# A hybrid decoder layer on one core: index scores in three float32r products, the lead in halves, new ranks

## The chip, the cores and the metric

The kernel runs on one core of a Trainium2 chip. The metric is the device time of one execution in microseconds (us), taken as the median over runs. PE is the matrix engine TensorE, PEld its weight loads, DVE is VectorE, ACT is ScalarE, POOL is GpSimd, and SP issues the transfers.

## The reference, cut to what matters

One decoder layer over 1024 tokens of width 1024. The input is RMS-normalised, scaled and shifted by vectors computed from a conditioning vector `c`, and projected to 2888 columns. Half of the mixed width comes from a pooling mixer with windows 2, 4, 8 and 16, half from sparse attention: an indexer scores every key for every query, the 256 best keys are kept, and attention runs over those.

```python
mod = jnp.einsum('bd,de->be', jax.nn.silu(c), w_ada[l]) + b_ada[l]
shift, scale, gate = jnp.split(mod, 3, axis=-1)
h = rms_norm(x, norm_w[l]) * (1.0 + scale[:, None, :]) + shift[:, None, :]
proj = jnp.einsum('bsd,de->bse', h, w_in[l])
...
logits = jnp.einsum('bqhd,bsd->bqhs', qib, kf_idx) * (IDX_DIM ** -0.5)
score = jnp.einsum('bqhs,bqh->bqs', jax.nn.relu(logits), wb) * (N_IDX_HEADS ** -0.5)
score = jnp.where(causal[None], score, -jnp.inf)
_, sel = lax.top_k(score, k_top)
...
y = jnp.einsum('bse,ed->bsd', jnp.concatenate([pool_out, attn_out], axis=-1), w_out[l])
x = x + gate[:, None, :] * y
```

The indexer has 8 heads of 64 dimensions and one shared key. Queries 0 to 255 keep all their keys, so scores are computed for the query tiles 2 to 7 (128 queries each) alone.

## The kernel before

Every strand of work is a Python generator that yields instructions one by one. At build time a list scheduler (`Flow`) decides which strand's next instruction is issued to its engine; it goes by a model of each instruction's length and by ranks, the numbers in `EARLY`, `LAST` and `SAFE`, and by the order of the projection tiles in `ORDER`. Each engine then runs its instructions in that fixed order. `Either(...)` lets the scheduler choose the engine. A `bank` is one of eight PSUM banks of 512 columns; the constants `QK`, `IK`, `FK`, `PV` and `KEEP` say how many banks a strand must leave free. All instructions pass through one helper, so that they have one line number in the profile, and the names of tiles tell them apart.

Matmuls in float32 accuracy are made of three products in the single-pass type float32r: a tile is split in a high part (a rounded copy) and a low part (the rest), and high x high, low x high and high x low are added in PSUM. For the normalised input the parts are `hhi` and `hlo`, for the weights `wh` and `wl`. The index scores and the attention scores are an exception before the change: they are plain f32 matmuls over 64 dimensions (`kiT,qix` and `kT,qr`), two heads at a time, one on the upper and one on the lower 64 rows of the array.

In the order of time:

1. Squares of the input blocks (`sq`) are summed over the width by 64 one-column matmuls (`c,sq`). `token_scales` makes of them one factor for each token, spread over all partitions (`rsb`). DVE computes `scale` and `shift` by products with accumulation (`wa`), each followed by a small operation on a column (`c<-c`).
2. The lead (`lead_line`): the eight input blocks are normalised on the fly (`xn`, `hhi`, `hlo`, by `h_block`), and each is multiplied with its chunk of weights as soon as it is there. The key/value matmuls (`wkh`, `wkl`) follow.
3. `index_keys` turns the index keys (`kiT`); `index_scores` issues the score matmuls, ACT takes their relu (`kt<-m`, a ring of two tiles), DVE sums them with the head weights (`score`). The other projections (`etile`: `hhi,wh`, `hhi,wl`, `hlo,wh`, 512 columns each) fill PE between them.
4. The 256th largest score of each query is found by bisection over 16-bit keys: DVE does it for the query tiles 2 to 4 (one round is three counts `junk`, a compare `aq` and a step `xq`), ACT for 5 to 7 (`ajunk`). Meanwhile DVE sums shifted copies `nx` for the pooling mixers, whose results `u` PE multiplies (`u,c`), and `qsh`/`qsl` split the queries for their norms.
5. Attention: scores `kT,qr`, masked maxima (`ex`, `mx`), exponentials, transposes (`c,ex`, `pw`), products with the values (`pw,vrow`). The output projections (`mph`, `mpl` for the mixers, `mah`, `mal` for attention) fill PE.

Of the kernel before, what the change touches and what calls it, by code (L numbers as in the profile page):

```python
# [17 lines left out]
P = 128  # L18
# [9 lines left out]
ORDER = "a2 a0 a1 q1 q2 | q0 m1 q3 m3 m2 m0 a3"  # L28
SWAP16 = [(i + 16) % 32 for i in range(32)]
WARM = [()] * 8  # L30
# [8 lines left out]
EARLY = {"main": 0.6, "fill": 0.4, "weights": 0.0, "evac": -1.0, "side": 0.2, "h": -0.2, "mods": -0.2,  # L39
         "select": -0.1, "scores": -0.6, "attend": -1.1, "late": 1.0, "kv": -0.3, "qi": -0.8, "pick": -0.6,  # L40
         "mix": -0.36, "rotated": -0.18, "query_loads": 0.01, "exps": -0.11, "score_sums": -1.13,
         "key_value_out": -0.58, "index_queries": -1.39, "norm": -2.29, "gate_loads": -0.03, "token_scales": -0.31,
         "gate_mods": 0.58, "unit": -0.41, "index_scores": -0.39, "lead_loads": 1.53, "out": -1.53, "lead_out": -0.72,
         "weight_loads": -0.1, "key_value_weights": -0.24, "main_line": 1.04, "output_line": 0.3, "turns": -1.82,
         "finish": -0.62, "index_keys": -0.9, "h_block": -0.1, "attention_keys": -0.68, "turned": -1.72,
         "h_blocks": -0.05, "gated": -1.24}

SELECT = -0.461
LAST = {"main": 0.12, "fill": 0.129, "scores": 0.008}

SAFE = {"side": 1.0, "unit": 0.1, "query_norms": 0.67, "rotated": 0.7, "norm": 0.45, "weight_loads": 0.1}

SCALED = (0,)
# [3 lines left out]
WKM = 4  # L57
# [3 lines left out]
PHOP = -0.008  # L61
STT = 0.062
HOPS = {"PE": 0.19, "DVE": 0.13, ("ACT", "DVE"): 0.14, ("ACT", "ACT"): 0.035}

SWITCH = {"all": 0.1, "rows": 0.25, "columns": 0.32}
# [3 lines left out]
PW_POOL = 0.4  # L69
XO_POOL = 0.45  # L70
BACK = 0.5
SPAN = 0.5

QK = 4
IK = 4
FK = 2
# [3 lines left out]
KEEP = 6  # L80
# [3 lines left out]
PV = 2  # L84

WA_AHEAD = 5
AHEAD = 3
XN_AHEAD = 2

FAVOUR = {"DVE": 0.122, "ACT": -0.13, "POOL": 0.013}  # L90
# [9 lines left out]
class Op:  # L100
# [29 lines left out]
    def _cost(self, aps, kw):  # L130
# [5 lines left out]
        if eng == "PE":  # L136
            rate = 2 if self.name == "transpose" else 4 if aps[1].dtype == F32 else 1
            if rate == 4 and min(aps[0].shape[0], aps[1].shape[0]) == 64:
                self.mode = "rows" if aps[1].shape[0] == 64 else "columns"
                rate = 2  # L140
            return max(0.109, size[0] * 0.000417 * rate + 0.0135)
# [128 lines left out]
class Flow:  # L270
# [3 lines left out]
    def __init__(self):  # L274
# [5 lines left out]
        self.strands = []  # L280
# [47 lines left out]
    def spawn(self, gen, kind="side"):  # L328
        s = [gen, EARLY.get(gen.__name__, EARLY[kind]), None, kind]
# [45 lines left out]
def hybrid_layer(ctx, tc, xT, cT, nwT, badaT, wada, wq, wet, wkv, qnw, knw, wpool,  # L375
# [79 lines left out]
    sc = const([P, 8], F32)  # L455
    rs = const([P, 8], F32)
# [1064 lines left out]
```

## Time and profile before

| what | value |
|---|---|
| median of 3 runs | 534.77 us (533.91 to 534.86) |
| profiled execution: time | 535.14 us |
| profiled execution: span | 533.2 us |
| PE busy | 510.2 us, 96% of the span |
| DVE busy | 427.3 us, 80% |
| ACT busy | 376.4 us, 71% |
| POOL busy | 160.5 us, 30% |

The span is the time from the first to the last instruction that the trace records; 1.9 us of the profiled execution lie around it. PE counts as busy for nearly the whole span, but busy time is counted at whatever clock is granted, so a stretch at half clock counts as busy too.

### The profile page before, as it was taken

Reading aid. Unit: us, or ns where it says so; the run is one execution under the profiler, and the core shown is the slowest. Engines: PE = TensorE matmul, PEld = TensorE weight load, DVE = VectorE, ACT = ScalarE, POOL = GpSimd, SP = SyncE. Lnnn points to the kernel's source line nnn. Section 1 sums busy time; section 2 is a strip of 40 time slices with the busy share of each in tenths; the row PEclk is TensorE's granted clock in tenths of the full one; section 3 lists DMA queues with packets and bytes.
Section 4 is the critical chain, followed back from the end, with each engine's and each line's share of the span. In section 5 each row is a group of like instructions: output and inputs, shape, how many; then the busy total and the mean of one; then the engine's idle time right before and its main releaser. Section 6 shows DMA issues by size and latency. Waiting matters only on the chain.

```text
span 533.2 us, 7630 instructions
## 1 busy us (share of the span) xinstructions
PE 510.2 (96%) x2492; PEld 378.2 (71%) x2492; DVE 427.3 (80%) x895; ACT 376.4 (71%) x848; POOL 160.5 (30%) x173
## 2 busy tenths in 40 slices
PE   5969999999999999999999797999999999999997
PEld 5758899755657887878878575876585856636575
DVE  0699996699886899999999899798856999886142
ACT  6357731487878888999962789799999834796420
POOL 1298240000000345555246147243202423100000
PEclk9979999999999999999999798899999999999999
DMA  8995418202011111121110014465252723301044
GB/s 307 405 408 167 136 48 297 79 0 80 21 61 59 41 41 41 39 71 49 36 44 20 21 60 125 131 188 182 69 177 81 227 90 100 98 20 41 1 157 158
DMA packets 28023, 58.29 MB, mean 109 GB/s; under 512 B 3792, under 2 KB 7888, under 8 KB 27984
## 3 DMA queue, kind: packets, MB, share of 16 engines
q1 hardware_dynamic: 27984, 57.81, 31.8%
q8 instruction: 19, 0.31, 0.3%
q14 instruction: 20, 0.16, 0.1%
HBM read 47.32 MB, written 10.49 MB: 108 GB/s over the span
## 4 chain that ended last, share of the span: by engine, by line
PE 55%; DVE 31%; ACT 6%; issue 5%; DMA 1%; POOL 1%; SPq 0%; DVEq 0%; POOLq 0%
PE m L196 55%; DVE junk L196 9%; ACT ex L196 4%; DVE ex L196 3%; DVE selw L196 3%; DVE aq L196 2%; DVE nx L196 1%; DVE sw L196 1%; DVE xq L196 1%; DVE key L196 1%; DVE wa L196 1%; DVE u L196 1%; DVE hlo L196 1%; DVE qr L196 1%; DVE gp L196 1%
## 5 line engine op out<-in xcount | busy, mean ns | idle before, releaser
L196 PE MATMUL m<-hhi,wh 128*128 128x512 f32 (+1 forms) x320 | 120.8, 399 | 0.5 <-ACT hhi L196 0.5
L196 PE MATMUL m<-hlo,wh 128*128 128x512 f32 (+1 forms) x320 | 114.8, 383 | 4.5 <-DVE hlo L196 4.5
L196 PE MATMUL m<-hhi,wl 128*128 128x512 f32 (+1 forms) x320 | 115.7, 383 | 0.0
L196 ACT ACTIVATE ajunk<-key,xq 128x768 bf16<-128x768 uint16 (+2 forms) x93 | 96.4, 1037 | 4.9 <-DVE xq L196 3.6
L196 PEld LDWEIGHTS m<-hhi,wh 128*128 128x128 f32 x320 | 59.6, 191 | 21.0 <-issue 7.4
L196 POOL TENSOR_TENSOR wl<-ld,wh 128x512 fp32r<-128x512 f32 x40 | 61.6, 1542 | 33.8 <-ACT wh L196 15.3
L196 PEld LDWEIGHTS m<-hlo,wh 128*128 128x128 f32 x320 | 59.2, 190 | 16.9 <-DVE hlo L196 5.2
L196 DVE TENSOR_SCALAR_CACHE_REDUCE junk<-key,xq 128x384 bf16<-128x384 uint16 (+2 forms) x93 | 69.1, 743 | 2.2
L196 PEld LDWEIGHTS m<-hhi,wl 128*128 128x128 f32 x320 | 59.5, 191 | 12.9 <-issue 1.9
L196 ACT ACTIVATE ex<-ex,mx,c 128x256 f32<-128x256 f32 (+7 forms) x64 | 54.8, 858 | 2.2 <-DVE mx L196 2.1
L196 ACT ACTIVATE kt<-m 128x512 f32<-128x512 f32 (+1 forms) x80 | 38.0, 523 | 13.3 <-DVE score L196 9.5
L196 DVE SCALAR_TENSOR_TENSOR score<-kt,c,score 128x1024 f32<-128x1024 f32 (+5 forms) x42 | 39.9, 950 | 6.7 <-ACT kt L196 4.8
L196 PE MATMUL m<-kT,qr 64*128 64x512 f32 (+3 forms) x192 | 39.0, 515 | 3.5 <-DVE mx L196 3.5
L196 DVE CUSTOM_DVE_ANT_0 ex<-m,key 128x512 f32<-128x512 f32 (+1 forms) x48 | 30.9, 661 | 6.3 <-PE m L196 6.3
L196 PEld LDWEIGHTS m<-c,ex 128*128 128x128 f32 x288 | 31.7, 140 | 5.9 <-ACT ex L196 2.8
L196 PE MATMUL m<-c,ex 128*128 128x128 f32 x288 | 35.1, 275 | 0.8 <-ACT ex L196 0.8
L196 DVE SCALAR_TENSOR_TENSOR xo<-m,c,xo 128x512 f32<-128x512 f32 x23 | 17.0, 740 | 22.6 <-PE m L196 22.3
L196 PEld LDWEIGHTS m<-kT,qr 64*128 64x128 f32 x192 | 18.2, 188 | 22.6 <-issue 12.2
L196 PE MATMUL m<-pw,vrow 128*64 128x512 f32 x144 | 33.5, 601 | 0.0
L196 PE MATMUL m<-kiT,qix 64*128 64x512 f32 (+3 forms) x160 | 32.2, 532 | 0.0
L196 POOL TENSOR_SCALAR_AFFINE_SELECT score<-score 128x128 f32<-128x128 f32 x6 | 3.1, 510 | 91.1 <-PE m L196 46.5
L196 ACT CAST wh<-ld 128x512 fp32r<-128x512 f32 x35 | 21.4, 617 | 11.2 <-PE m L196 11.2
(182 smaller groups left out, 1050.7 us busy)
## 6 DMA issues: line engine op xcount, KB each, us to landing
wa<-wada SPq DMA_DIRECT2D x24, 512.0 KB, 7.5
ld<-wet SPq DMA_DIRECT2D x16, 512.0 KB, 3.3
ld<-wout SPq DMA_DIRECT2D x24, 256.0 KB, 2.8
xo<-xT SPq DMA_DIRECT2D x16, 256.0 KB, 3.3
y_d<-xo SPq DMA_DIRECT2D x16, 256.0 KB, 2.3
xo<-y_d SPq DMA_DIRECT2D x16, 256.0 KB, 3.0
outT<-xo SPq DMA_DIRECT2D x16, 256.0 KB, 2.1
xt<-xT SPq DMA_DIRECT2D x7, 512.0 KB, 6.9
```

Of the source, the lines that this page charges most:

```text
L196: self.fn(*self.args, **self.kw)
```

## The change

Three things change together. First, index queries and index keys are split in high and low parts (`split` on the queries gives `xh` and `xl`; `turn_split` gives two tiles `kiT`), and each f32 score matmul becomes three float32r products (`dots`), issued alternately for the two row groups. Second, in the lead the token sums go to two banks, one for each half of the tokens, with scales per half; the first block is normalised in halves (`first_block`), the small column operations become strands of their own that may run on ACT or DVE (`gear`, `shift`), and two filler matmuls (`xt,c`) go. Third, ranks, model constants and bank reserves get new values, many ranks per instance of a strand.

```diff
-ORDER = "a2 a0 a1 q1 q2 | q0 m1 q3 m3 m2 m0 a3"
+ORDER = "a0 a2 a1 q1 q2 | q0 m1 q3 m2 m3 m0 a3"
...
-SCALED = (0,)
...
+SCALED = ()
...
-WKM = 4
+WKM = 5
...
-QK = 4
-IK = 4
-FK = 2
+QK = 3
+IK = 3
+FK = 0
...
-KEEP = 6
+KEEP = 7
...
-PV = 2
+PV = 3
...
-AHEAD = 3
+AHEAD = 2
...
-        s = [gen, EARLY.get(gen.__name__, EARLY[kind]), None, kind]
+        name = gen.__name__
+        n = self.spawned[name] = self.spawned.get(name, 0) + 1
+        s = [gen, EARLY.get(f"{name} {n}", EARLY.get(name, EARLY[kind])), None, kind]
...
+        halves = [slice(512, 1024), slice(0, 512)]
+        tab["sums"] = []
+        for _ in range(2):
+            tab["sums"].append((yield bank(4)))
+        added = [j for j in range(NT) if j not in SUMS]
+        acc, started = None, set()
         for j in range(NT):
             sq = yield big(s="sq")
-            for c in ([slice(0, 512), slice(512, 1024)] if j == NT - 1 else [slice(0, 1024)]):
+            for c in (halves if j == NT - 1 else [slice(0, 1024)]):
                 yield A.activation(sq[:, c], xt[j][:, c], AF.Square)
-                if acc is not None and j not in SUMS:
+                if j in added and acc is not None:
                     yield V.tensor_tensor(acc[:, c], acc[:, c], sq[:, c], op=OP.add)
-                if j == NT - 1 or j in SUMS:
+                if j in SUMS or j == added[-1]:
                     t = sq if j in SUMS else acc
-                    for b in range(c.start // P, c.stop // P):
-                        yield mm(ps_r[:, b:b + 1], t[:, b * P:(b + 1) * P], ones, j == SUMS[0] and b == 0,
-                                 j == NT - 1 and b == NT - 1)
+                    for h, half in enumerate(halves):
+                        if half.start >= c.start and half.stop <= c.stop:
+                            for b in range(4):
+                                o = half.start + b * P
+                                yield mm(tab["sums"][h][:, b:b + 1], t[:, o:o + P], ones,
+                                         h not in started, j == NT - 1 and b == 3)
+                                started.add(h)
...
+        for h, r in enumerate((rs[:, 4:8], rs[:, 0:4])):
+            yield A.activation(r, tab["sums"][h], AF.Sqrt, scale=1.0 / 1024.0, bias=eps_sb)
+            flow.drop(tab["sums"][h])
+            yield V.reciprocal(r, r)
+            ps = yield bank()
+            yield Group([PE.transpose(ps[:, b * P:(b + 1) * P], r[:, b:b + 1].to_broadcast([P, P]), ident)
                          for b in range(4)])
-        tab["ps_b"] = ps_b
-        for half in range(2):
-            yield A.copy(rsb[:, half * 512:(half + 1) * 512], ps_b[half])
+            rsbs.append(ps)
...
+            yield V.scalar_tensor_tensor(ada[j][0], ada[j][0], 1.0, tab["scp"], op0=OP.mult, op1=OP.mult, accum_out=g)
             flow.drop(ada[j][0])
-            yield V.tensor_scalar(gs[:, j:j + 1], m, bada_sb[:, 8 + j:9 + j], nw_sb[:, j:j + 1],
-                                  op0=OP.add, op1=OP.mult)
-            geared.append(j)
-            yield from modulation(ada[j][1], tab["scp"], j)
-            modded.append(j)
+            flow.spawn(gear(j, g), "mods")
+            yield V.scalar_tensor_tensor(ada[j][1], ada[j][1], 1.0, tab["scp"], op0=OP.mult, op1=OP.mult, accum_out=m)
+            flow.drop(ada[j][1])
+            flow.spawn(shift(j, m), "mods")
...
+    def gear(j, g):
+        yield Either(A.activation(gs[:, j:j + 1], g, AF.Identity, scale=nw_sb[:, j:j + 1], bias=bnw[:, j:j + 1]),
+                     V.tensor_scalar(gs[:, j:j + 1], g, bada_sb[:, 8 + j:9 + j], nw_sb[:, j:j + 1],
+                                     op0=OP.add, op1=OP.mult))
+        geared.append(j)
+
+    def shift(j, m):
+        b = bada_sb[:, j:j + 1]
+        yield Either(A.activation(m, m, AF.Identity, bias=b), V.tensor_scalar(m, m, b, None, op0=OP.add))
+        modded.append(j)
...
+    def first_block():
+
+        xn = yield big(s="xn")
+        hi = yield big(F32R, s="hhi")
+        lo = yield big(F32R, s="hlo")
+        g, m = gs[:, 0:1], mod_sb[:, 0:1]
+
+        def low(n, c):
+            yield V.scalar_tensor_tensor(lo[:, c], xn[:, c], m, hi[:, c].bitcast(F32), op0=OP.add, op1=OP.subtract)
+            lo_in.append((0, n))
+            hlo[0] = lo
+            if len(lo_in) == 2:
+                flow.drop(xn)
+
+        for n, c in enumerate((slice(512, 1024), slice(0, 512))):
+            yield lambda: len(rsbs) > n and 0 in geared
+            yield V.scalar_tensor_tensor(xn[:, c], xt[0][:, c], g, rsbs[n], op0=OP.mult, op1=OP.mult)
+            yield lambda: 0 in modded
+            yield A.activation(hi[:, c], xn[:, c], AF.Identity, bias=m)
+            hi_in.append((0, n))
+            hhi[0] = hi
+            flow.spawn(low(n, c), "h")
+        flow.drop(xt[0])
+        yield lambda: "rsb" in tab
+        flow.drop(*rsbs)
...
-            acc[len(acc), 0] = yield bank()
-            yield mm(acc[len(acc) - 1, 0], ident, xt[NT - 1][:, :512], True, True)
         for j in range(NT):
             whi, wlo = yield from take_chunk()
-            yield lambda: j in hhi
             turns = [(k, c, range(4)) for k, c in ((0, 0), (1, 0), (0, 1), (1, 1), (2, 0), (2, 1))]
             if j == NT - 1:
                 turns = [(k, c, (e,)) for e in range(4) for c in (0, 1) for k in (0, 1, 2)]
             for k, c, es in turns:
-                if k == 2:
-                    yield lambda: j in hlo
+                yield lambda: (j, c) in (lo_in if k == 2 else hi_in)
...
-        qi[e] = x
+        qi[e] = yield from split(x, 768)
...
+    def turn_split(rows, hi, lo):
+
+        for c in (slice(0, 512), slice(512, 1024)):
+            ps = yield bank()
+            yield Group([PE.transpose(ps[:, b * P:(b + 1) * P], rows[:, c][:, b * P:(b + 1) * P], ident)
+                         for b in range(4)])
+            yield hi_of(hi[:, c], ps)
+            yield lo_of(lo[:, c], ps, hi[:, c])
+            flow.drop(ps)
+
+    def split(x, w):
+
+        hi = yield big(F32R, w, "xh")
+        lo = yield big(F32R, w, "xl")
+        yield hi_of(hi, x)
+        yield lo_of(lo, x, hi)
+        flow.drop(x)
+        return hi, lo
+
+    def dots(ps, q, k, r, qs, ks):
+
+        return [mm(ps, a[r, qs], b[r, ks], n == 0, n == 2)
+                for n, (a, b) in enumerate(((q[0], k[0]), (q[1], k[0]), (q[0], k[1])))]
...
-        t2 = yield big(s="kiT")
-        yield from turn(twice, t2)
+        both = []
+        for _ in range(2):
+            both.append((yield big(F32R, s="kiT")))
+        yield from turn_split(twice, *both)
         flow.drop(twice)
-        ki["T"] = t2
+        ki["T"] = both
...
-                        ops.append(mm(ps[:, :c1 - c0], qi[e][r, i * P - 256:(i + 1) * P - 256],
-                                      ki["T"][r, c0:c1], True, True))
+                        ops.append(dots(ps[:, :c1 - c0], qi[e], ki["T"], r, slice(i * P - 256, (i + 1) * P - 256),
+                                        slice(c0, c1)))
                         put.append((c0, c1, ps))
-                yield Group(ops)
+                yield Group([o for a, b in zip(ops[::2], ops[1::2]) for both2 in zip(a, b) for o in both2])
```

In `EARLY` there are 86 more names than before, such as `"norm 3": -3.08` or `"out 13": -1.6`; `SAFE` and `LAST` are filled in the same way.

In the lead both programs are re-ordered too. On DVE the first half of the first `xn` has two reciprocals, three `wa` and a column operation ahead of it after the change, before it one reciprocal, two `wa` and a column operation. On ACT the second half of the first `hhi` followed the first half directly; now `hhi` and `xn` of the second block, a cast and two column operations stand between the two.

PE, index scores of the first query tile (7), in program order before: `kiT` is the turned key tile, `qix` a tile of two heads' queries, `x4` stands for four matmuls in a row (two row groups, two halves of 512 keys).

```order
295 L196 MATMUL m<-hhi_283,wh_600 128x512
296 L196 MATMUL m<-hhi_283,wl_601 128x512
297 L196 MATMUL m<-hlo_284,wh_600 128x512
298 L196 MATMUL m<-kiT_942,qix_607 128x512 x4
299 L196 MATMUL m<-kiT_942,qix_608 128x512 x4
300 L196 MATMUL m<-kiT_942,qix_632 128x512 x4
301 L196 MATMUL m<-hhi_324,wh_600 128x512
302 L196 MATMUL m<-hhi_324,wl_601 128x512
```

The same place after; `xh` and `xl` are the high and low parts of the queries, the two `kiT` numbers the high and low parts of the keys.

```order
299 L216 MATMUL m<-hhi_362,wh_620 128x512
300 L216 MATMUL m<-hhi_362,wl_621 128x512
301 L216 MATMUL m<-hlo_363,wh_620 128x512
302 L216 MATMUL m<-kiT_947,xh_684 128x512 x2
303 L216 MATMUL m<-kiT_947,xl_727 128x512 x2
304 L216 MATMUL m<-kiT_948,xh_684 128x512 x2
305 L216 MATMUL m<-kiT_947,xh_684 128x512 x2
306 L216 MATMUL m<-kiT_947,xl_727 128x512 x2
307 L216 MATMUL m<-kiT_948,xh_684 128x512 x2
308 L216 MATMUL m<-kiT_947,xh_770 128x512 x2
```

Each group of four became twelve in steps of two, one for each row group.

PE, from the last projection product before the first attention scores, in program order before: `kT` is the turned key tile, `qr` a tile of two heads' queries, `mph`, `mpl` the mixers' parts in the output projection.

```order
1096 L196 MATMUL m<-hlo_558,wh_2845 128x512
1097 L196 MATMUL m<-kT_1465,qr_1696 128x128 x2
1098 L196 MATMUL m<-kT_1465,qr_1438 128x128 x2
1099 L196 MATMUL m<-kT_1465,qr_1696 128x256 x2
1100 L196 MATMUL m<-kT_1465,qr_1564 128x128 x2
1101 L196 MATMUL m<-kT_1465,qr_2086 128x128 x2
1102 L196 MATMUL m<-kT_1465,qr_1438 128x256 x2
1103 L196 MATMUL m<-kT_1465,qr_1564 128x256 x2
1104 L196 MATMUL m<-kT_1465,qr_2086 128x256 x2
1105 L196 MATMUL m<-mph_3150,wh_2961 128x512
1106 L196 MATMUL m<-mph_3150,wl_2962 128x512
1107 L196 MATMUL m<-mpl_3151,wh_2961 128x512
```

And after:

```order
1179 L216 MATMUL m<-hlo_548,wh_3005 128x512
1180 L216 MATMUL m<-kT_1661,qr_1839 128x128 x2
1181 L216 MATMUL m<-kT_1661,qr_1588 128x128 x2
1182 L216 MATMUL m<-kT_1661,qr_1839 128x256 x2
1183 L216 MATMUL m<-kT_1661,qr_1712 128x128 x2
1184 L216 MATMUL m<-kT_1661,qr_1588 128x256 x2
1185 L216 MATMUL m<-mph_3297,wh_3097 128x512
1186 L216 MATMUL m<-mph_3297,wl_3098 128x512
1187 L216 MATMUL m<-mpl_3298,wh_3097 128x512
1188 L216 MATMUL m<-mph_2462,wh_3097 128x512
1189 L216 MATMUL m<-mph_2462,wl_3098 128x512
1190 L216 MATMUL m<-mpl_2463,wh_3097 128x512
```

Sixteen score matmuls stood together before the first projection product; after, ten stand before it, and six more follow behind twelve products.

DVE, at the end of the score sums and before the first bisection, before: `key` are 16-bit keys, `qsh` and `qsl` parts of a query tile.

```order
160 L196 TENSOR_TENSOR wl_1435<-ld_1120,wh_1434 128x512
161 L196 COPY key_88<-kt_1442 128x1024
162 L196 MEMSET xq_250_1483 128x3
163 L196 COPY kT_1465<-m 128x512
164 L196 CAST qsh_1436<-st_1510 128x512
165 L196 TENSOR_TENSOR qsl_1437<-st_1510,qsh_1436 128x512
```

The same place after: `wa` is one of the products that make the output gate.

```order
142 L216 COPY key_86<-kt_1591 128x768
143 L216 SCALAR_TENSOR_TENSOR score_1458<-kt_1616,c_101,score_1458 128x384
144 L216 SCALAR_TENSOR_TENSOR score_1458<-kt_1626,c_101,score_1458 128x384
145 L216 SCALAR_TENSOR_TENSOR wa_1585,c_89<-wa_1585,scb_484 128x1024
146 L216 CAST qsh_1586<-st_1639 128x512
147 L216 TENSOR_TENSOR qsl_1587<-st_1639,qsh_1586 128x512
148 L216 SCALAR_TENSOR_TENSOR score_1458<-kt_1631,c_101,score_1458 128x384
149 L216 TENSOR_SCALAR c_89<-c_89,c_78 128x1
```

A `wa` product stands among the last score sums now and with it a small column operation, where before it was ahead of all of them; four such `wa` are behind the first score sum after the change and none before.

## Rows read from the trace of the kernel before

**Rows 1.** The page: busy us (share of the span) and instructions of each engine.

```profile
PE 510.2 (96%) x2492; PEld 378.2 (71%) x2492; DVE 427.3 (80%) x895; ACT 376.4 (71%) x848; POOL 160.5 (30%) x173
```

**Rows 2.** What PE waited for: us in total, times, longest.

```profile
PE m L196 <- DVE hlo L196: 4.5, 2, 2.8
PE m L196 <- DVE mx L196: 3.5, 2, 1.8
PE m L196 <- DVE u L196: 2.8, 1, 2.8
```

**Rows 3.** Timeline of PE in the lead: start us, us, instructions, idle before.

```profile
26.87 1.19 PE L196 MATMUL m<-hhi,wh 128*128 128x512 f32 x4 [0.49 <-ACT hhi L196]
...
36.66 1.91 PE L196 MATMUL m<-hhi,wh 128*128 128x512 f32 x4
...
67.48 0.32 PE L196 MATMUL m<-wkh,hhi 128*128 128x328 f32 x1
```

**Rows 4.** Stretches: length, then PE, PEld, DVE, ACT, POOL busy (instructions), PE's granted clock, DMA.

```profile
36.00:38.00 2.00, 2.00 (x8) 1.71 (x8) 2.00 (x3) 1.97 (x2) 2.00 (x2) 0.50 1.04 416
...
300.00:306.00 6.00, 6.00 (x11) 3.48 (x11) 4.63 (x13) 2.35 (x9) 0.23 (x1) 0.50 0.02 9
330.00:336.00 6.00, 4.79 (x12) 3.46 (x13) 5.96 (x29) 4.45 (x13) 2.17 (x2) 0.50 0.52 162
```

**Rows 5.** Timeline of PE around one group of index scores.

```profile
118.12 0.39 PE L196 MATMUL m<-hhi,wh 128*128 128x512 f32 x1
...
118.57 0.39 PE L196 MATMUL m<-hlo,wh 128*128 128x512 f32 x1
118.89 1.77 PE L196 MATMUL m<-kiT,qix 64*128 64x512 f32 x8
120.59 0.50 PE L196 MATMUL m<-hhi,wh 128*128 128x512 f32 x1
```

**Rows 6.** Timeline of PE at the third mixer input and the first attention scores.

```profile
299.98 2.08 PE L196 MATMUL m<-u,c 128*128 128x512 f32 x2 [2.78 <-DVE u L196]
...
324.30 1.37 PE L196 MATMUL m<-kT,qr 64*128 64x128 f32 x16
327.36 2.02 PE L196 MATMUL m<-kT,qr 64*128 64x128 f32 x12 [1.70 <-DVE mx L196]
331.21 1.43 PE L196 MATMUL m<-kT,qr 64*128 64x256 f32 x4 [1.83 <-DVE mx L196]
```

**Rows 7.** What DVE waited for from 100 to 180 us.

```profile
DVE score L196 <- ACT kt L196: 7.0, 15, 1.9
DVE qsh L196 <- ACT st L196: 3.3, 2, 3.0
```

**Rows 8.** Longer stretches, columns as in rows 4.

```profile
160.00:180.00 20.00, 20.00 (x94) 16.08 (x93) 13.84 (x32) 18.38 (x41) 2.29 (x3) 1.00 0.11 40
180.00:340.00 160.00, 153.56 (x654) 119.97 (x653) 152.07 (x356) 126.08 (x302) 78.09 (x89) 0.96 0.16 52
```

**Rows 9.** The tile `aq`: duration ns min/median/max, first and last start.

```profile
L196 DVE TENSOR_TENSOR aq<-cq,kcq x31: 147/163/1843, 181.0 to 338.7; 128x3 f32<-128x3 f32 x31
```

**Rows 10.** Groups of DVE: busy us, mean ns of one, idle before.

```profile
L196 DVE TENSOR_TENSOR wl<-ld,wh 128x512 fp32r<-128x512 f32 x24 | 16.8, 702 | 0.1
...
L196 DVE SCALAR_TENSOR_TENSOR wa<-wa,scb 128x1024 f32<-128x1024 f32 x8 | 9.8, 1219 | 5.0 <-DMA wa<-wada 5.0
...
L196 DVE TENSOR_TENSOR nx<-u 128x1023 f32<-128x1023 f32 x4 | 5.2, 1302 | 0.0
...
L196 DVE CAST qsh<-st 128x512 fp32r<-128x512 f32 x2 | 0.9, 428 | 3.3 <-ACT st L196 3.3
```

**Rows 11.** Groups of DVE in one bisection round; `junk` stands three times in a round.

```profile
L196 DVE TENSOR_SCALAR_CACHE_REDUCE junk<-key,xq 128x384 bf16<-128x384 uint16 (+2 forms) x93 | 69.1, 743 | 2.2
...
L196 DVE TENSOR_TENSOR aq<-cq,kcq 128x3 f32<-128x3 f32 x31 | 16.8, 542 | 0.6
...
L196 DVE SCALAR_TENSOR_TENSOR xq<-aq,yq 128x3 f32<-128x3 f32 x29 | 8.1, 279 | 2.0
```

More of the change, by code (lines that the diff above doesn't have):

```diff
@@ L36 @@
 ROOM = {"b": 36, "ld": 2, "st": 3, "wh": 4, "wl": 4, "kt": 2, "sg": 2, "selw": 1, "m": 8}
[L39 to L46, printed above, removed]
@@ new lines @@
+SELECT = -0.366
+LAST = {"main": 0.12, "fill": 0.113, "scores": -0.039, "attend": -0.078, "evac": -0.027, "qi": 0.284,
+        "side": -0.239}
+SAFE = {"side": 1.0, "unit": 0, "query_norms": 0, "h_block": 0.59, "rotated": 0.73, "query_loads": 0,
+        "norm": 0.0, "weight_loads": 1.18, "key_value_out": 0.39, "turned": 0.26, "finish": 0.07, "index_keys": 0,
+        "main_line": 0, "output_line": 0, "gate_mods": 1.07, "selection": 0, "low": 0, "maxima": 0,
+        "attention": 0.05, "lead_out": 0, "score_relus": 0.1, "lead_loads": 0.28, "score_sums": 0.18, "mix": 0.96,
+        "main": 0, "modulations": 0.09, "out": 0.39, "turns": 0, "exps": 0}
@@ L55 @@
+SCALED = ()
 SUMS = (0,2,4,)
-WKM = 4
+WKM = 5
 HOP = 0.103
-PHOP = -0.008
-STT = 0.062
+PHOP = -0.09
+STT = 0.075
 HOPS = {"PE": 0.19, "DVE": 0.13, ("ACT", "DVE"): 0.14, ("ACT", "ACT"): 0.035}
-SWITCH = {"all": 0.1, "rows": 0.25, "columns": 0.32}
+SWITCH = {"all": 0.1, "rows": 0.29, "columns": 0.29}
 AGE = 0.37
-PW_POOL = 0.4
-XO_POOL = 0.45
+PW_POOL = 0.303
+XO_POOL = 0.108
 BACK = 0.5
-SPAN = 0.5
-QK = 4
-IK = 4
-FK = 2
+SPAN = 0.115
+QK = 3
+IK = 3
+FK = 0
 PK = 0
 MIX = 4
-KEEP = 6
+KEEP = 7
@@ L82 @@
 FLY = 2
-PV = 2
+PV = 3
 WA_AHEAD = 5
-AHEAD = 3
+AHEAD = 2
 XN_AHEAD = 2
-FAVOUR = {"DVE": 0.122, "ACT": -0.13, "POOL": 0.013}
+FAVOUR = {"DVE": 0.235, "ACT": -0.057, "POOL": 0.244}
 TABLES = {AF.Silu: 1, AF.Sqrt: 2, AF.Exp: 3}
@@ L455, in hybrid_layer @@
     sc = const([P, 8], F32)
+    bnw = const([P, 8], F32)
     rs = const([P, 8], F32)
@@ L666, in lead_line @@
         pair = {}
-        for _ in range(2):
-            acc[len(acc), 0] = yield bank()
-            yield mm(acc[len(acc) - 1, 0], ident, xt[NT - 1][:, :512], True, True)
         for j in range(NT):
             whi, wlo = yield from take_chunk()
-            yield lambda: j in hhi
             turns = [(k, c, range(4)) for k, c in ((0, 0), (1, 0), (0, 1), (1, 1), (2, 0), (2, 1))]
```

85 lines of the change are left out of this document (37 added, 48 removed), and 12 rows, old and new, of the table EARLY.

## Prediction

> **What bounds the kernel now.** I began with the busy times. TensorE (PE) is busy for 510.2 of 533.2 us and VectorE (DVE) for 427.3 [rows 1], so almost every us of PE work counts, unless PE would then only wait longer. The list of PE's waits says for whom: after the opening there are three that matter, 4.5 us for `hlo` in the lead, 2.8 us for `u`, the input of a pooling mixer, and 3.5 us for `mx`, the row maxima of the first attention scores [rows 2]. All three are waits for DVE.
>
> The lead starts at 26.87, its second chunk at 36.66, and the key/value matmuls behind its eight chunks at 67.48 [rows 3]: 40.6 us. A chunk has 12 products of 512 columns and 12 of 256. One of 512 takes 0.225 us from start to start (two in 118.12 to 118.57) [rows 5], so a chunk needs 12 x 0.225 and 12 times half of it, 4.05 us, and eight need 32.4. Some 8 us are lost, 4.5 of them in the waits, the rest at a low clock: at 36 to 38 us the granted clock is 0.50, the 1.2 GHz level, after PE had twice waited [rows 4].
>
> In the middle DVE is the tight engine. From 180 to 340 us it is busy for 152.07 of 160, and PE, though behind hundreds of ready matmuls, for 153.56 [rows 8]. Here PE waits 2.78 us for `u` (to 299.98) and 1.70 and 1.83 us for `mx` [rows 6], and after each of the two places the clock is 0.50 for six us (300 to 306, 330 to 336) [rows 4]. Six us at half clock do the work of three, so the two places cost 6.3 + 6.0 = 12.3 us. Ahead of that stretch DVE has room: from 160 to 180 it is busy for 13.84 of 20 [rows 8], and in 100 to 180 it waits 7.0 us for the relus `kt` and 3.3 for an evacuated query [rows 7]. From the start of the attention scores (324.30) [rows 6] PE has matmuls nearly to the end; there it sets the time.
>
> **The change, part by part.** *Index scores.* A group of four program matmuls of 512 columns (8 in the trace, f32 taking two each) runs from 118.89 to 120.59 [rows 5]: 1.70 us, or 0.85 for a pair on the two row groups. That is 4 x 4 passes x 512 columns / 2 row groups / 2.4 GHz = 1.71 us: both row groups run at once and no weight load shows. There are 33 pairs' worth of columns (8 heads x 4224 columns / 1024). After, a pair is three float32r products per row group. No float32r product on 64 rows is in this trace. If the row groups overlap as they do for f32, a pair costs 3 x 0.225 = 0.675 us, and 33 x (0.85 - 0.675) = **-5.8 us** of PE. At the other end, without overlap, 6 x 0.225 = 1.35 us, **+16.5 us**. I take the first, because the loads can keep up: in the narrow attention scores 16 trace matmuls of 128 columns, each with its own load, pass in 1.37 us [rows 6], 0.086 us each, and the new pair asks for six loads in 0.68.
>
> The Trainium skill, "TensorE: Matmul & The Clock Gate", Part 3, says that a weight load overlaps matmuls in flight only when its row group differs. In the order a0, b0, a1, b1 the next load for a row group would by that rule wait for the product on it; then a pair is 3 x (0.225 + 0.086) = 0.93 us and the index scores cost +2.7 us. The f32 group of 1.70 us speaks against it, since it too reloads each row group several times and shows no gap.
>
> *The lead.* Both DVE and ACT are re-ordered. The first half's sums are ready before the second half's, but on DVE both reciprocals and three `wa` of 1.2 us [rows 10], one more than before, stand ahead of the first `xn`, so I give the start of the lead only 1 us. The second half's `hhi` now stands behind `hhi` and `xn` of the next block and a cast on ACT: about 3 us by lengths like that of `wa`, so a wait of about 3 us takes the place of 4.5. The sum is **-2.5 us**, bounds -0.5 (the 1.0 and 1.5 are mostly eaten by a clock that falls earlier, since the two filler matmuls `xt,c` are gone) and -4.5 (both waits vanish). Those two only filled waiting time and save nothing by going.
>
> *DVE.* Six more `etile` products (6 x 0.225 = 1.4 us) stand ahead of the first index score, so DVE begins its score sums 1.4 - 2.5 = 1.1 us earlier. Counted from there to the first row maximum, DVE gets four gate `wa` (4 x 1.22 = 4.9), six `qsh` casts from GpSimd (6 x 0.43 = 2.6), two more shifted sums `nx` (2.4; 1.30 with its contention, I take 1.2), four `wl` (2.8), four small operations (0.8) and an `mph` cast (0.8, twice the `qsh` of half its width). It loses two casts (-0.9) and two bisection rounds that now come later: a round is 3 x 0.74 + 0.54 + 0.28 = 3.05 us, so -6.1 [rows 10, 11]. Sum: **+7.3 us** of DVE work ahead of the first maximum. To the third `u` only one round is left behind, there are three more `nx` (3.6) and three, not four, `wl`: 4.9 + 2.6 + 3.6 + 2.1 + 0.8 - 0.9 - 3.05 = **+10 us**.
>
> What hides it: the idle time of DVE in 100 to 180. The waits named are 10.3 us; one `wa` stands right where the 3.0 us wait for the query was, the other work stands between score sums. Bounds: 3 us absorbed (that one place), or all 10.3. And DVE meets GpSimd less: the 128x3 compare `aq` has a median of 163 ns, a longest of 1843 [rows 9] and a mean of 542 [rows 11], so 31 x 0.38 = 11.7 us are lost beside GpSimd's 89 instructions of that stretch [rows 8]. Eight of those leave GpSimd (six `qsh`, two long `mpl`): 8/89 x 11.7 = 1.1, and I take 1.5 since two are long; below, nothing.
>
> So the third `u` comes at -1.1 + 10 - 1.5 - (3 to 10.3), that is +4.4 to -2.9, middle +0.8; the first maximum at -1.1 + 7.3 - 1.5 - (3 to 10.3), that is +1.7 to -5.6, middle **-2.0 us**.
>
> *PE at the attention scores.* By its own work PE would be 5.8 + 2.5 = 8.3 us early. At the third `u` DVE does not let it: 18 more `etile` products now stand between second and third `u` (4.1 us), so PE, which waited 2.8, will wait about 2.8 + 8.3 - 4.1 + 0.8 = 7.8 us there. The gain of the index scores is spent in that wait, and PE goes on with DVE's -2.0.
>
> *Order behind it.* Before, 16 attention-score matmuls stood together and PE waited twice; after, 10, then 12 projection products, then 6. The first wait stays, the second (1.83 us) [rows 6] gets work in its place, and half of the three us behind it that the half clock took should go too: 1.8 + 1.5 = **-3.3 us**. Bounds: nothing (if `mpl`, two of which move to DVE at about 1.3 us each, is late for those products) and -3.5 - 3.0 = -6.5.
>
> Sum for the likeliest: -2.0 - 3.3 = -5.3 us. The profiled execution took 535.14 us (span 533.2 and 1.9 around it), 0.4 above the median of the runs shown. 534.8 - 5.3 = **529.5 us**, own range 526 to 533.
>
> **Rivals.** *PE sets the time.* DVE absorbs all its added work, and all 8.3 us arrive: with the 3.3 that is -11.6, or -12.3 with part of the first `mx` wait: 522.5. For it: DVE's idle 6 us at 160 to 180. Against it: 152 of 160 busy behind it.
>
> *Nothing passes.* DVE's middle stretch holds PE, only 3 us are absorbed (+1.7), and 1.8 come back from the filled wait: 534.7, no change. The Trainium skill's "TensorEngine Tiling (Array Packing)", section "PSUM Bottleneck", says that packing speeds TensorE but not the evacuation, which may become the limit. By it the index stage would gain nothing, since ACT's relus and DVE's sums, not PE, set its length; its own time would be this rival's. The 7.0 us of DVE's waits for `kt` [rows 7] agree that those two engines pass the stage between them.
>
> *Slower.* DVE's 7.3 us find no idle place before the attention scores, and GpSimd's going gives nothing back: the first maximum comes at -1.1 + 7.3 = +6.2, and the filled wait returns 1.8 to 3.3: +2.9 to +4.4, 538.5. It decides as soon as less than about 4 us of DVE's added work are hidden, because all of PE's work behind the maxima then starts later.
>
> *The products don't pack.* With loads exposed (0.93 us a pair) PE is 0.2 us later, not 8.3 earlier; DVE's -2.0 is then out of reach, and the fill gives about 532 to 534. With no overlap at all PE is 14 us late: 548.
>
> **How the numbers follow.** Likeliest 0.45; PE sets 0.20; nothing passes 0.12; slower 0.17; no packing 0.06 (half of it slower, half small gains). The runs shown lie within 0.2% (1.1 us), about what a measurement can tell from no change. Faster: 0.45 + 0.20 + a little of the last = 0.66; same 0.12; slower 0.22, the rest of the likeliest's upper edge among it. The range 522 to 537 leaves out the lower half of the second case, the upper half of the fourth and the packing that fails outright: 0.10 + 0.08 + 0.02. The likeliest alone is 526 to 533.
>
> **What would show it.** A group of twelve 64-row products of 512 columns in 1.35 to 1.45 us shows the packing right; 1.9 shows exposed loads, 2.7 no overlap. The lead should end near 65. PE's wait for `u` should grow from 2.8 to about 7.8 us, and the attention scores should start about 2 us earlier (322), not 8. Of the waits for `mx` one should be left. If PE's `u` wait is under 3 us and the attention scores start near 316, DVE was not the limit and the time is near 522. If DVE's first score sum is not earlier than before, the lead was mis-sized.

## The result and the profile after

The changed kernel takes 526.31 us (median of 4 runs, 525.81 to 527.01) beside 534.34 us for the kernel before (4 runs, 532.85 to 534.86): ratio 0.9855, 95% interval 0.983 to 0.988. In a second group of runs, on which the last experiments stand, it was again 526.31 us, beside 531.25 for the kernel before: ratio 0.9896, 0.9871 to 0.9922. The profiled execution has a span of 524.1 us, 9.1 less than before. The profiled execution of the kernel before (535.14 us, mean granted clock 0.98) is among the slowest of that kernel, whose others go down to 528.9 us at 0.99, so differences between the two traces overstate what the change gives.

The page of the changed kernel, busy times first, then the granted clock in 40 slices:

```profile
PE 500.9 (96%) x2568; PEld 380.8 (73%) x2568; DVE 421.7 (80%) x902; ACT 381.7 (73%) x868; POOL 134.9 (26%) x154
...
PEclk9999999999999999999999997999999999999999
```

PE is still busy for 96% of the span. Its busy time fell by 9.3 us against [rows 1], as much as the span, so PE is idle for as long as before (some 23 us). The largest of the waits that the change touches:

```profile
PE m L216 <- ACT hhi L216: 4.0, 2, 2.7
PE m L216 <- DVE u L216: 1.8, 2, 1.5
PE m L216 <- DVE mx L216: 1.5, 1, 1.5
PE m L216 <- DVE mpl L216: 1.5, 1, 1.5
```

Against [rows 2], the two waits for `hlo` (4.5 us) are gone and two for `hhi` are there (4.0): 2.67 us ahead of the lead, where the fillers stood, and 1.30 inside it. The waits for `u` went from 2.8 to 1.8, those for `mx` from 3.5 to 1.5, and a wait for `mpl` is new. Together these are 2 us shorter (10.8 to 8.8); other waits that are new, for `mah` on DVE (1.2) and `qsh` (0.8), make up for it. The lead, on PE's timeline:

```profile
25.41 2.08 PE L216 MATMUL m<-hhi,wh 128*128 128x512 f32 x4 [2.67 <-ACT hhi L216]
...
30.30 0.74 PE L216 MATMUL m<-hhi,wh 128*128 128x256 f32 x4 [1.30 <-ACT hhi L216]
...
33.03 1.08 PE L216 MATMUL m<-hhi,wh 128*128 128x512 f32 x4
...
62.57 0.32 PE L216 MATMUL m<-wkh,hhi 128*128 128x328 f32 x1
```

It starts at 25.41 (before 26.87), its second chunk at 33.03 (36.66), and the key/value matmuls at 62.57, 4.9 us earlier than in [rows 3]. One group of index scores, with the last product ahead of it and the first behind:

```profile
104.63 0.40 PE L216 MATMUL m<-hlo,wh 128*128 128x512 f32 x1
104.96 0.50 PE L216 MATMUL m<-kiT,xh 64*128 64x512 f32 x2
105.29 0.40 PE L216 MATMUL m<-kiT,xl 64*128 64x512 f32 x2
105.53 0.62 PE L216 MATMUL m<-kiT,xh 64*128 64x512 f32 x4
105.99 0.39 PE L216 MATMUL m<-kiT,xl 64*128 64x512 f32 x2
106.22 0.39 PE L216 MATMUL m<-kiT,xh 64*128 64x512 f32 x2
106.54 0.50 PE L216 MATMUL m<-hhi,wh 128*128 128x512 f32 x1
```

Twelve products take 1.58 us (104.96 to 106.54). Inside the group two products, one on each row group, pass every 0.23 us; the rest of the 1.58, some 0.2 us, is the change to 64 rows and back.

The group of 1.70 us in [rows 5] is not the same work. The timeline names only the first shape of a row; sorted by shape, half of that group's matmuls have 384 columns, so it is a group of 896 keys and not of 1024:

```profile
L196 PE MATMUL m<-kiT,qix x8: 482/536/694, 118.9 to 120.2; 64*128 64x512 f32 x4, 64*128 64x384 f32 x4
```

A group of 1024 keys in f32 takes 1.92 us, as the run with f32 scores in the order of after shows (first experiment below; all eight of these matmuls have 512 columns):

```profile
105.72 1.99 PE L879 MATMUL m<-kiT,xh 64*128 64x512 f32 x8
107.64 0.50 PE L216 MATMUL m<-hhi,wh 128*128 128x512 f32 x1
```

Added up on PE's timeline, from the start of each row of index products to the next other matmul, the index products take 31.3 us before, 27.4 after, and 31.9 in f32 in the order of after. The changed order has 17 such stretches where the old one had 13, each with its change to 64 rows and back.

The third mixer input, the last one, the first attention scores and the first output products:

```profile
296.04 1.02 PE L216 MATMUL m<-u,c 128*128 128x512 f32 x2
...
306.42 1.98 PE L216 MATMUL m<-u,c 128*128 128x512 f32 x4 [0.27 <-DVE u L216]
...
313.81 1.37 PE L216 MATMUL m<-kT,qr 64*128 64x128 f32 x16
316.65 0.91 PE L216 MATMUL m<-kT,qr 64*128 64x256 f32 x4 [1.47 <-DVE mx L216]
...
319.69 0.80 PE L216 MATMUL m<-mpl,wh 128*128 128x512 f32 x1 [1.47 <-DVE mpl L216]
...
324.26 1.98 PE L216 MATMUL m<-kT,qr 64*128 64x256 f32 x12
```

At the third mixer input, where PE had waited 2.78 us, it does not wait at all (296.04, without a wait behind it). The attention scores start at 313.81, 10.5 us earlier than in [rows 6], and PE waits for one set of maxima instead of two. Then it waits 1.47 us for `mpl`, and from 320 on products of 512 columns follow each other at 0.43 us. The clock says why (columns as in [rows 4]):

```profile
36.00:38.00 2.00, 2.00 (x12) 1.68 (x12) 1.89 (x4) 1.87 (x3) 2.00 (x2) 1.00 1.01 403
308.00:310.00 2.00, 2.00 (x9) 1.46 (x9) 1.93 (x7) 1.97 (x4) 0.00 (x0) 1.00 0.74 188
320.00:322.00 2.00, 2.00 (x6) 1.54 (x6) 2.00 (x8) 0.00 (x0) 0.00 (x0) 0.50 0.49 162
180.00:340.00 160.00, 154.21 (x668) 120.52 (x667) 149.89 (x357) 129.59 (x322) 54.58 (x73) 0.98 0.21 66
```

At 36 to 38 us the clock is 1.00 now, where it was 0.50. Behind the last mixer input (308 to 310) it is 1.00, where behind the third one it had been 0.50 for six us (300 to 306) [rows 4]. At 320 to 322 it is 0.50, as it was at 330 to 336 before. Of the three stretches at half clock in [rows 4], one is left. From 180 to 340 DVE is busy for 149.89 us (before 152.07) with 357 instructions (356), and GpSimd for 54.58 (before 78.09) [rows 8]. The compare `aq`, whose mean was 542 ns [rows 11]:

```profile
L216 DVE TENSOR_TENSOR aq<-cq,kcq 128x3 f32<-128x3 f32 x31 | 7.8, 253 | 0.5
```

### The profile page after: what moved, and what is told of

Its sections match the earlier page's. It is cut to its first block, busy times and chain, and to the rows that moved or that the text cites. A ratio compares the mean times of both kernels' runs of the same rounds, so it can differ in the third digit from the quotient of the medians.

```text
span 524.1 us, 7765 instructions
## 1 busy us (share of the span) xinstructions
PE 500.9 (96%) x2568; PEld 380.8 (73%) x2568; DVE 421.7 (80%) x902; ACT 381.7 (73%) x868; POOL 134.9 (26%) x154
## 4 chain that ended last, share of the span: by engine, by line
PE 61%; DVE 26%; ACT 7%; issue 4%; POOL 1%; DMA 1%; SPq 0%; DVEq 0%; ACTq 0%
PE m L216 61%; DVE junk L216 10%; ACT ex L216 3%; DVE selw L216 2%; DVE nx L216 2%; DVE sw L216 2%; DVE xq L216 1%; DVE ex L216 1%; DVE aq L216 1%; ACT ajunk L216 1%; DVE gp L216 1%; DVE wl L216 1%; DVE qr L216 1%; DVE mpl L216 1%; DVE u L216 1%
## 5 line engine op out<-in xcount | busy, mean ns | idle before, releaser
L216 POOL TENSOR_TENSOR wl<-ld,wh 128x512 fp32r<-128x512 f32 x38 | 54.0, 1423 | 43.7 <-ACT wh L216 35.5
L216 ACT ACTIVATE ex<-ex,mx,c 128x384 f32<-128x384 f32 (+7 forms) x64 | 54.9, 859 | 6.5 <-DVE mx L216 6.4
L216 DVE SCALAR_TENSOR_TENSOR xo<-m,c,xo 128x512 f32<-128x512 f32 x28 | 21.0, 748 | 24.6 <-PE m L216 19.7
L216 PE MATMUL m<-kT,qr 64*128 64x512 f32 (+3 forms) x192 | 37.9, 512 | 1.6 <-DVE mx L216 1.5
L216 ACT CAST wh<-ld 128x512 fp32r<-128x512 f32 x36 | 22.0, 615 | 16.3 <-PE m L216 10.8
L216 POOL TENSOR_SCALAR wh<-ld 128x512 fp32r<-128x512 f32 x23 | 15.7, 683 | 69.1 <-PE m L216 58.1
L216 PE MATMUL m<-mah,wh 128*128 128x512 f32 x64 | 25.8, 404 | 2.5 <-ACT mah L216 1.3
```

The source lines that it names most:

```text
L216: self.fn(*self.args, **self.kw)
```

## The experiments

Seven of the runs keep the order of every engine as the changed kernel or the kernel before has it and change only what an instruction does when it is issued, so that the scheduler moves nothing else; an eighth turns twelve products of PE round and keeps the rest. Three plan anew, and one is the changed kernel again. The kernel before had medians of 531.46, 533.54 and 531.25 us in the three groups of runs, so kernels of different groups are compared by their ratios to it.

**f32 index scores in the order of after.**

```diff
+        ops[0].fn = lambda out, a, b, start, stop: nc.tensor.matmul(out, a.bitcast(F32), b.bitcast(F32),
+                                                                    start=True, stop=True)
+        ops[1].fn = ops[2].fn = lambda *args, **kw: None
```

> The order of all engines is that of the changed kernel; only the index score products are put back: one f32 matmul of the high parts instead of three float32r products (the low parts are still made, but not multiplied, so the scores lack them). Theory 1, PE sets the time in the index stage and what it saves there arrives at the end: the 5.8 us of PE come back, 531 to 533 us. Theory 2, as the prediction had it, VectorE holds PE at the third mixer input: PE's wait for u shrinks instead, 526 to 528 us.

Measured: 531.24 us, ratio to the kernel before 0.9989 (0.9966 to 1.0012). Against the changed kernel's 0.9896 that is 0.9%, some 4.9 us back. On PE's timeline the attention scores start 4.7 us later than in the changed kernel:

```profile
318.55 1.37 PE L216 MATMUL m<-kT,qr 64*128 64x128 f32 x16
```

The score sums on DVE show how it gets there (duration ns min/median/max, first and last start); this run, then the changed kernel:

```profile
L216 DVE SCALAR_TENSOR_TENSOR score<-kt,c,score x42: 609/946/1286, 104.1 to 168.1; 128x1024 f32<-128x1024 f32 x7, 128x896 f32<-128x896 f32 x7, 128x768 f32<-128x768 f32 x7, 128x640 f32<-128x640 f32 x7
```

```profile
L216 DVE SCALAR_TENSOR_TENSOR score<-kt,c,score x42: 610/946/1285, 103.7 to 163.6; 128x1024 f32<-128x1024 f32 x7, 128x896 f32<-128x896 f32 x7, 128x768 f32<-128x768 f32 x7, 128x640 f32<-128x640 f32 x7
```

The last sum starts at 168.1 instead of 163.6. DVE's own work in the middle begins 4.5 us later when the index products take longer. PE's wait for `u` is 1.7 us in this run and 1.8 in the changed kernel; theory 2 had it shrink. So what PE saves in the index scores is not lost in waits for DVE: DVE moves with it. Theory 1 holds. At the end of this execution only 2.3 us of the 4.7 are left (span 526.4): the clock stays at 1.00 behind `mpl`, where the changed kernel's fell to 0.50. By the medians it is 4.9.

**One product of the three.**

```diff
+        ops[0].fn = lambda out, a, b, start, stop: nc.tensor.matmul(out, a, b, start=True, stop=True)
+        ops[1].fn = ops[2].fn = lambda *args, **kw: None
```

> The order is that of the changed kernel; of the three index products only high x high is issued, so PE is relieved of another 2 x 33 x 2 products on two row groups, about 15 us (the scores lack the two correction products). Theory 1, PE still sets the time: 511 to 514 us. Theory 2, VectorE is close behind: only a few us arrive, 521 to 525 us, and PE's waits for u and mx grow by some 10 us.

Measured: 524.34 us, ratio 0.9854 (0.9812 to 0.9896): of 15 us of PE's work some 2 arrive. The tile `kiT` in this run, and what the wait ahead of its instructions ended on (weight loads and matmuls):

```profile
L879 PE MATMUL m<-kiT,xh x80: 217/441/502, 101.8 to 154.6; 64*128 64x512 f32 x48, 64*128 64x384 f32 x16, 64*128 64x256 f32 x8, 64*128 64x128 f32 x8
...
  ACT kt L216: 17.8, 37
```

The last index product starts at 154.6, one us earlier than the 155.6 of the changed kernel (the lead of this execution had ended 1.4 us later), and PE or its weight loads now stand 37 times for the relus `kt`, which wait for DVE's sums. The waits for `u` and `mx` did not grow (1.8 and 2.0 us), so the loss is not where theory 2 had put it. With three products PE's length of the stage and that of ACT and DVE are within some 2.4 us of each other; with f32 PE was the longer. The Trainium skill's "TensorEngine Tiling (Array Packing)", section "PSUM Bottleneck", says that packing does not speed the evacuation, which may become the limit: this run shows that limit, and that the change stops just at it.

**Low parts twice on GpSimd, in the order of after.**

```diff
+        if low and 10 <= flow.lows < 26:
+            self.fn(*self.args, **self.kw)
         self.fn(*self.args, **self.kw)
```

> The order is that of the changed kernel; the 16 low parts of weights that GpSimd makes between 170 and 325 us are each made twice, with the same result (about 21 us more of GpSimd work, so that it is as busy there as before the change). Theory 1, GpSimd's instructions with two inputs hold up VectorE's: the mean of the compare aq goes from 0.25 to 0.4 us or more, VectorE reaches the attention maxima 4 to 8 us later, 529 to 533 us. Theory 2, GpSimd's load does not matter to VectorE: 526 to 527 us, aq as it was.

Measured: 536.57 us, ratio 1.0078 (1.0049 to 1.0107), 1.8% or nearly 10 us above the changed kernel. PE's wait for `u`, the compare `aq`, and the start of the attention scores in this run:

```profile
PE m L221 <- DVE u L221: 8.1, 3, 5.2
```

```profile
L221 DVE TENSOR_TENSOR aq<-cq,kcq 128x3 f32<-128x3 f32 x31 | 13.0, 420 | 0.5
```

```profile
325.82 1.37 PE L221 MATMUL m<-kT,qr 64*128 64x128 f32 x16
```

`aq` takes 420 ns on average instead of 253, PE waits 8.1 us for `u` instead of 1.8, and the attention scores start 12 us later (1.1 of it in a lead that ended later in this execution). DVE's order and work are the same. GpSimd is busy for 74.9 us from 180 to 340 in this run, nearly the 78.09 of before [rows 8]. That GpSimd's load alone does this is shown; how much of it is DVE being held and how much the low parts themselves coming later is not separated here, but no wait of PE for `wl` appears.

**Blank low parts in the order of before.**

```diff
+        if low and 10 <= flow.lows < 31:
+            flow.blank(self.args[0].bitcast(F32))
+        else:
+            self.fn(*self.args, **self.kw)
```

> The order is that of the kernel before; the 21 low parts of weights that GpSimd makes between 170 and 325 us are written as zeros by GpSimd, without reading anything (so these low parts are left out of the products). Theory 1, as in the run with the parts made twice: the mean of aq falls from 0.54 to 0.3 us or less, VectorE comes 5 to 10 us earlier to the third mixer input and the first maxima, PE's waits for u and mx (6.3 us) mostly go, with the half clock behind them: 525 to 530 us. Theory 2: 533 to 535 us.

Measured: 526.39 us, ratio 0.9907 (0.9877 to 0.9937). The counterpart on the kernel before: 5 us without touching PE, DVE or their order.

```profile
L202 DVE TENSOR_TENSOR aq<-cq,kcq 128x3 f32<-128x3 f32 x31 | 10.4, 335 | 0.6
```

```profile
316.35 3.20 PE L202 MATMUL m<-kT,qr 64*128 64x128 f32 x28
322.32 0.91 PE L202 MATMUL m<-kT,qr 64*128 64x256 f32 x4 [2.77 <-DVE mx L202]
```

The mean of `aq` falls to 335 ns. PE waits for `u` no more, and the attention scores start at 316.35 instead of 324.30 (1.6 of it is a lead that ended earlier in this execution); one wait for `mx` is left, and grew to 2.77 us.

The Trainium skill, "SBUF — State Buffer", section "Who interferes with whom", says that a DVE instruction with two SBUF inputs contends with a GpSimd instruction that reads SBUF, not with one that only writes, and that the later of the two waits for the other's end. Both runs agree with it: `aq` has two such inputs, longest 1.84 us [rows 9] against a median of 0.16, and zeros that are only written hold it up less. But a blank is also shorter (mean 0.54 us, a low part 1.50), so reading and length are not separated here.

**Both at once: f32 index and low parts twice.** The two edits above together, in the order of after.

> The changed kernel's order with both the f32 index matmul and the low parts made twice on GpSimd. If VectorE, held up by GpSimd, sets the time as the prediction had it, the f32 index adds nothing to the run with the low parts made twice: its ratio is again about 1.008. If the two costs add, 1.008 + 0.0135, about 1.02.

Measured: 539.65 us, ratio 1.0148 (1.0122 to 1.0175), 0.7% above the run with the low parts made twice. The attention scores:

```profile
327.31 1.37 PE L221 MATMUL m<-kT,qr 64*128 64x128 f32 x16
```

1.5 us later than with the low parts alone (2.6 if one allows for a lead that ended 1.1 us earlier in this execution), where the f32 index had cost 4.7. Neither expectation is met exactly: with GpSimd as busy as before, part of PE's saving is lost and part still arrives.

**No fillers in the order of before.**

```diff
-            yield mm(acc[len(acc) - 1, 0], ident, xt[NT - 1][:, :512], True, True)
+            filler = mm(acc[len(acc) - 1, 0], ident, xt[NT - 1][:, :512], True, True)
+            filler.fn = lambda *args, **kw: None
+            yield filler
```

> The kernel before in its own order without the two filler matmuls xt,c at 21 to 26 us. If they only fill waiting time, the same time, 533.5 to 535 us; if they keep the clock up, the lead runs at half clock earlier and ends 1 to 2 us later: 535 to 537 us.

Measured: 530.16 us, ratio 0.9964 (0.9929 to 0.9999): a little faster, barely clear of no change, which neither alternative had. PE's timeline and two stretches:

```profile
21.63 1.97 PE L196 MATMUL m<-c,c 128*128 128x128 f32 x8 [0.59 <-DVE c L196]
25.67 2.07 PE L196 MATMUL m<-hhi,wh 128*128 128x512 f32 x4 [2.08 <-ACT hhi L196]
...
32.80 1.09 PE L196 MATMUL m<-hhi,wh 128*128 128x512 f32 x4
...
64.91 0.32 PE L196 MATMUL m<-wkh,hhi 128*128 128x328 f32 x1
```

```profile
24.00:26.00 2.00, 0.33 (x1) 0.33 (x2) 2.00 (x5) 1.21 (x2) 1.36 (x2) 1.00 1.04 416
36.00:38.00 2.00, 2.00 (x12) 1.71 (x11) 1.97 (x4) 0.82 (x1) 2.00 (x2) 1.00 1.04 414
```

The transposes of the token factors `c,c` start at 21.63 instead of 22.88, since no filler stands ahead of them, `hhi` comes 1.2 us earlier, and the lead ends at 64.91 instead of 67.48. Two executions are a thin base for these 2.6 us: in the run with blank low parts, which is the kernel before up to its first blank at 174 us, fillers and all, the lead ended at 65.88, 1.0 us later than without. PE stands nearly idle at 24 to 26 us, and yet the clock is 1.00 at 36 to 38 us, where it was 0.50 with the fillers. What the fillers do give is a faster start: the lead's first four products last 2.07 us without them, 1.19 with them [rows 3]. Without them they start 0.47 us apart, near the 0.43 of the half clock at 320 us in the changed kernel, although the clock column reads 1.00 there.

**No fillers and blank low parts, in the order of before.**

> The kernel before in its order, without the two fillers and with the 21 low parts of weights written as zeros (left out of the products). If the two effects are separate they add: 0.9964 and 0.9907 give about 0.987. If the lead's 2.6 us are lost again in waits for VectorE, about 0.991.

Measured: 525.13 us, ratio 0.988 (0.9852 to 0.9909). The middle of the interval is where the two effects would add (0.9964 x 0.9907 = 0.987); its upper end touches the 0.991 at which the lead's part would be lost, so this run favours the sum and does not prove it.

**Code without the new ranks.** Three kernels plan anew: the lead alone, the index products alone, and both, each with the ranks and numbers of the kernel before.

> The changed lead (sums and first block in halves, small column operations as strands, no fillers) with the ranks and numbers of the kernel before and the f32 index scores. The scheduler plans anew. If the code of the lead gives its gain, the key/value matmuls start 3 to 5 us earlier than 67.5 and the time is 530 to 532 us; if the new ranks give it, they start near 67 and the time is 533 to 536 us.

> The kernel before with the index products in float32r alone; its ranks and numbers and its lead stay. Theory 1, PE's saving arrives: 528 to 531 us. Theory 2, VectorE, whose work and beside it GpSimd's are those of before, holds PE at the mixers: 533 to 535 us and PE's waits for u and mx grow from 6.3 to 10 us or more.

> The changed lead and the changed index products with the ranks and numbers of the kernel before. If the ranks only arrange what the two code changes give, 526 to 529 us; if the ranks (which engine makes what, GpSimd relieved) are needed for the gains to arrive, 530 to 534 us.

Measured: 560.8 us (ratio 1.0549, 1.0495 to 1.0603), 572.94 us (1.0768, 1.07 to 1.0836) and 714.9 us (1.3444, 1.3364 to 1.3525). None of the expected figures is near. Every plan is a new order, with waits of its own (in the last, one wait of PE for `kt` of 152.5 us), so these runs say nothing of what the lead or the products are worth; they say only that the old ranks don't serve the new code. How much of the gain the ranks give by themselves stays open.

**The changed kernel again, and its high products first.** In the first group of twelve output products the eight with high parts go ahead of the four with `mpl`; the sum is the same.

> The changed kernel itself, as the reference of this group on the same chip: a ratio near 0.9855 to the kernel before.

```diff
-                for q in range(2):
-                    yield accumulate(ps, w, hi, lo, (2 * q, 2 * q + 1))
+                pair = [accumulate(ps, w, hi, lo, (2 * q, 2 * q + 1)) for q in range(2)]
+                if dt == 0 and c == 0:
+                    highs_first(pair[0].ops + pair[1].ops)
+                yield pair[0]
+                yield pair[1]
...
+    def highs_first(ops):
+        put = [(o.fn, o.args) for o in ops]
+        turn = [3 * k + t for k in range(4) for t in range(2)] + [3 * k + 2 for k in (1, 2, 0, 3)]
+        for n, (o, m) in enumerate(zip(ops, turn)):
+            o.fn = lambda *args, fn=put[m][0], own=put[m][1], n=n, **kw: fn(*own, start=n == 0, stop=n == 11)
```

> The changed kernel; of the first group of twelve output products for the mixers the eight with high parts are issued first and the four with mpl last, so that PE has work while VectorE makes mpl. If the wait for mpl (1.47 us) and the half clock behind it (319 to 325 us, 3 us) are what the first attention scores still cost, 1.5 to 4 us less than the changed kernel; if VectorE's maxima set the time behind them, no difference.

Measured: 526.31 us (0.9896, 0.9871 to 0.9922) and 524.33 us (0.986, 0.9834 to 0.9886). The intervals to the kernel before touch, but the runs themselves lie at 524.98 to 526.70 and 523.28 to 525.12: 2 us, the best of the kernels here that leave nothing out. In the second kernel PE's last `mpl` product, and the clock:

```profile
319.38 0.86 PE L1431 MATMUL m<-mpl,wh 128*128 128x512 f32 x3
320.77 0.50 PE L1431 MATMUL m<-mpl,wh 128*128 128x512 f32 x1 [0.53 <-DVE mpl L216]
321.20 0.70 PE L216 MATMUL m<-kT,qr 64*128 64x256 f32 x4
```

```profile
320.00:322.00 2.00, 1.38 (x7) 0.49 (x5) 2.00 (x8) 0.69 (x2) 0.00 (x0) 1.00 0.31 114
```

The wait is 0.53 us instead of 1.47, the clock stays at 1.00, and the next attention scores start at 321.20 instead of 324.26.

## Why the prediction was right in its time and wrong in its steps

The time, 526.31 us, lies in the range of 522 to 537, and nearer to the forecast 529.5 than to the rival "PE sets the time" at 522.5. But the trace says that the rival's mechanism is what happened up to the attention scores. The prediction had named the sign of it: attention scores near 316, and PE's wait for `u` under 3 us. They are 313.81 and 1.8, and at the third `u`, where it forecast 7.8 us, PE does not wait.

*Index scores: right in kind, the row misread.* The row groups overlap, and no load is exposed: the mechanism that the prediction chose. By the rule of the Trainium skill ("TensorE: Matmul & The Clock Gate", Part 3) that it weighed against the row, with loads hidden only behind another row group, a group would have taken 1.9 us; it took 1.58, so the measurement decides against that reading of it. The row of 1.70 us, which the prediction took for four matmuls of 512 columns, has half of them at 384. Its sum of 1.71 us for 1024 columns leaves out the changes to 64 rows and back, so the two agreed by chance; a group of that size takes 1.92. The forecast of 1.35 to 1.45 leaves out the same changes, and since both sides carry the same 0.2 us, the saving per pair comes out nearly as forecast: (1.92 - 1.58) / 2 = 0.17 us against 0.175. Over the stage it is 3.9 us against the order of before and 4.6 in the same order, where 5.8 were forecast; the run with f32 scores gives 4.9 in the time.

*The lead: right in sign, too small.* 2.5 us were forecast with 4.5 as the far bound, 4.9 are in the two traces, and its end came at 62.57, not near 65. The wait inside the lead that was put at 3 us measured 1.30, and the half clock at 36 to 38 us, for whose going the prediction had no term, is gone. The failed sentence is that the fillers "only filled waiting time": without them the transposes start 1.25 us earlier, and the lead of the kernel before ends 1.0 to 2.6 us earlier. What the halves add to that was not run by itself.

*DVE in the middle: the step that failed.* The prediction laid 7.3 to 10 us of added work on DVE, counted 1.5 us for GpSimd, and let DVE hold PE at the third `u` for 7.8 us. Two terms were wrong. First, GpSimd's part was taken in proportion to its instructions, 8 of 89. In the stretch from 180 to 340 us 16 are gone (73 are left), four low parts `wl` among them, which the prediction had put on DVE without taking them off GpSimd; its busy time fell by 23.5 of 78 us. But even these shares of the 11.7 us give only 2.1 and 3.5, and the compare `aq` alone gave back 31 x (542 - 253) ns = 9.0 us. The two runs that change nothing but GpSimd's work move the time by +10 and -5 us. Second, DVE's start of the middle was taken as fixed but for the lead. It is not: DVE's sums wait for relus of PE's products, and with shorter products they end 4.5 us earlier than with f32 in the same order. So the gain of the index scores did not have to pass DVE; it moved DVE. Against the kernel before, the last sum starts 2.8 us earlier (166.4 there) and PE's last index product 5.0 us (160.6 there). The rest of the 10.5 us arises behind it: the wait of 2.78 us for the third `u` and the half clock behind that wait, some 3 us, are gone. Nor do 18 more `etile` products stand between the second and the third `u`, as the prediction counted, but 24 (1.4 us more).

*The order behind it: wrong sign.* 3.3 us were to come back behind the first attention scores. From there to the end the changed kernel loses 1.4 us (10.5 ahead at 313.81, 9.1 at the end). The filled wait for `mx` is gone, but `mpl`, which the prediction named as its lower bound, is late by 1.47 us, and the clock fell behind it as before. The run with the high products first shows that this was to be had: 2 us.

The two errors had opposite signs: 8.5 us too little ahead of the attention scores (-2.0 against -10.5) and 4.7 too much behind them (-3.3 against +1.4). That is why the sum came out near: by luck, and not because its steps held.

*The other rivals.* "Slower" did not happen, though the run with GpSimd kept busy shows its mechanism and its price: 536.6 us. "Nothing passes" is what the one-product run shows for any further saving in the index scores.

## What to carry to other kernels

Before calling one engine the bound of a stretch, ask what its first instruction there waits for: an engine that is saturated behind a stage moves as a whole when that stage ends earlier. Read the price of contention from the spread of a small, often repeated instruction (median against mean and maximum), and do not share it out by what leaves the other engine: neither its instructions nor its busy time gave the 9.0 us here. A run that changes that engine's work alone did. Before taking a timeline row as the price of a shape, ask for its shapes one by one; a row names only the first. And to test one cause in a kernel whose order is planned, keep the order and change what is issued; with a new plan the difference of plans is many times what is looked for.

## What had not been expected

A compare of 128x3 elements with a median of 0.16 us had a mean of 0.54, and 16 more GpSimd instructions in 150 us, none of whose results PE waited for, cost nearly 10 us: twice what the index products gave. And two matmuls that kept PE busy in front of the lead went with a half clock later in it, at 0.50 in 36 to 38 us; without them PE was busy for 0.33 of 2 us at 24 to 26, and the clock was 1.00 at 36 to 38. Which of the later gaps decided that, the runs do not tell: the waits for `hlo` were also shorter in the run without fillers.
